# First matrix of the last MLP as seven products of 256 columns, with its weight sums made during the second mixer

## The chip, the cores and the metric

The kernel runs on one core of a Trainium2 chip. The metric is the device time of one execution in microseconds (us). Lines such as L231 are lines of the kernel before, unless a sentence says otherwise; in the changed kernel the same code stands one line lower at L232, and further down by more.

The engines are named as the profile names them: PE multiplies matrices, DVE is the vector engine, ACT the scalar engine, POOL is hardly used here, and SP issues the DMAs. Each engine works through its own instructions in the order of the program, and an instruction that waits holds everything behind it on the same engine.

## The reference

A trunk of two layers works on 1024 tokens of width 1024 in fp32. Layer 0 mixes with a matrix memory (mLSTM), layer 1 with latent attention over shared keys and values; each is followed by an MLP of width 4096. Cut to what the change touches:

```python
h = modulate(rmsnorm(x, norm_g[l, 2]), sh2, sc2)      # h * (1 + scale) + shift
y = sqrelu_mlp(h, mlp_w1[l], mlp_w2[l])               # jnp.square(jax.nn.relu(h @ w1)) @ w2
x = x + g2[:, None, :] * rmsnorm(y, norm_g[l, 3])
```

`w1` is 1024 x 4096 and `w2` is 4096 x 1024.

## The kernel before

**Tiles and products.** The tokens go through in two halves of 512, `hfs[0]` and `hfs[1]`. Activations lie with the features on the 128 partitions, so a half is eight blocks `k` of 128 features by 512 tokens. Each fp32 operand is split into a rounded part and a remainder (type fp32r), and one product is three matmuls, low by high, high by low, high by high: `mm3`, L230 to L233. A weight tile is loaded by one DMA into `raw` (L211, 512 KB), cast on ACT to `wh` (L189), and its remainder is made by a subtraction on DVE, `wl` (L190). There are four `raw` buffers, and four pairs of `wh` and `wl`.

**The MLP.** `mlp` (from L967, before the change) makes a list of steps. A step `hidden(f)` makes 128 of the 4096 hidden features: eight `mm3`, that is 24 matmuls of 128 x 512, into one `ps` accumulator, then relu (L962) and square (L963) on ACT, and the split into `hd` (L471 on ACT, L472 on DVE). A step `up` multiplies hidden features by the second matrix: 24 matmuls of 512 columns into a `pm` accumulator, which DVE adds to the output (L198). The last MLP works in groups of four hidden features' blocks; the `up` steps of the group before alternate with the `hidden` steps of the next. Weights are asked for two steps ahead.

**What runs beside what.** The streams are laid out like this: the last layer's MLP on the first half, `mlp(1, hfs[0], ...)`, runs together with the second mixer, `mixer1(hfs[1], ...)`, which is latent, attention, output projection, residual and norm of the second half. Behind that the last MLP, `mlp(1, hfs[1], ...)`, runs alone but for a filler that writes the results out (`all_out`: `x_to_rows`, with transposes at L1577 and copies at L1578, and `rows_out`). `two_streams` interleaves the two generators; a scheduler then orders the instructions of each engine by a model of their times, with those under `high_priority` pulled ahead.

**Attention.** For each pair of heads and queries, PE makes scores into `pm` (L1330 to L1336), DVE takes the maximum (L1340, L1341), ACT the exponential (L1342), DVE the reciprocal and the scaling (L1343, L1344), PE turns the result (L1450) and multiplies by the values. Finished blocks go to DRAM as `oT` (L1471). Keys, queries and values come from DRAM into `k` tiles (L1427 to L1435), issued on SP among the weight loads.

**The end of the mixer.** `post` adds the residual, takes the norm, and `normed` writes the modulated half as eight pairs of high and low tiles (`Split`), one ACT and two DVE instructions for each feature block; the last MLP's products read them.

**Small buffers.** `tma` is a scratch tile of 2 KB for each partition with one buffer, `Cst` a constant tile that the second mixer doesn't read any more once its latent part is done, and `v8` a tile of layer 0 that lies idle in layer 1.

Of the kernel before, what the change touches and what calls it, by code (L numbers as in the profile page):

```python
# [9 lines left out]
F32 = mybir.dt.float32  # L10
# [7 lines left out]
P = 128  # L18
# [64 lines left out]
def kernel(  # L83
# [39 lines left out]
    def k4v(dt=F32, b=512):  # L123
        return k4(dt)[:, :1024].rearrange("p (a b) -> p a b", b=b)
# [104 lines left out]

    def mm3(o, lh, ll, rh, rl, start, stop):  # L230
        nc.tensor.matmul(o, ll, rh, start=start, stop=False)  # L231
        nc.tensor.matmul(o, lh, rl, start=False, stop=False)  # L232
        pe_last[0] = nc.tensor.matmul(o, lh, rh, start=False, stop=stop)  # L233

# [242 lines left out]
    def normed(h, xs_, rstd, A, sh):  # L477

        for k in range(KD):
# [5 lines left out]
            if k % 4 == 3:  # L485
                yield 1

    def along_tokens(dst, y):
# [143 lines left out]
    def qk_in(hf):  # L632
        hf.q = [k4v(), k4v()]
        hf.k = [k4v(), k4v()]
        for p_ in range(4):
# [3 lines left out]
            yield  # L639

    def v_in(hf):
        h = hf.h
        hf.v = []
        last = sb.tile([P, 4, VE], F32, tag="v8", bufs=1, name=f"v8_{next(uid)}")
        nc.gpsimd.memset(last[:, :, 128:VE], 1.0)
        for t in range(4):
# [298 lines left out]

    def mlp(l, hf, y, sizes, rows=False):


        w1, w2, h = mlp_w1[l], mlp_w2[l], hf.h2
        hids = {}  # L950

        def hidden(f):
# [645 lines left out]
    def rows_out(hf, y, B):  # L1598

        xt = []  # L1600
        for t in range(4):
            a = k4v()
            r0 = hf.i * H + t * P
            nc.sync.dma_start(a, xr[r0 : r0 + P, :].rearrange("p (a b) -> p a b", b=512))
            xt.append(a)
        yield
        for t in range(4):
            yt, st = y.t[t], small(4)
            for g in range(2):
                junk = ps()  # L1610
                nc.scalar.activation(junk, yt[:, g], AF.Square, accum_out=st[:, g : g + 1])
# [8 lines left out]
            for g in range(2):  # L1620
                nc.vector.scalar_tensor_tensor(ys[g], ys[g], r, xt[t][:, g], ALU.mult, ALU.add)
                r0 = hf.i * H + t * P
                nc.sync.dma_start(out[0, r0 : r0 + P, ts(g, 512)], ys[g])
            yield

# [129 lines left out]

    def post(hf, y, B, src, A, sh):
# [5 lines left out]
        yield 0  # L1762
        hf.h2 = Split()
        yield from normed(hf.h2, y, rstd, A, sh)
# [128 lines left out]


    z1 = FH(claim=True)
    ya = [None, None]

    def mixer1(hf, z, attention):
# [5 lines left out]
        yield "fill"  # L1904
        yield from lat
        yield next(att)
        yield from att
# [5 lines left out]
        yield 1  # L1913
        yield from post(hf, y, B2, x_cols, A3, adac(1, SH2))
# [6 lines left out]
    u1 = FH(claim=True)  # L1921

# [10 lines left out]
    v = None  # L1933
    dense = mlp(1, hfs[1], u1, [4] * 8, True)
    while (d := go(dense)) is not end:
# [32 lines left out]
```

## Time and profile before

| | |
|---|---|
| median of three runs | 2376.94 us (2375.88 to 2378.69) |
| the profiled execution | 2377.5 us, of which the span is 2375.5 us |
| granted TensorE clock, mean | 0.997 |
| PE busy | 2343.4 us in 11621 matmuls |
| DVE busy | 1549.6 us |
| ACT busy | 1055.6 us |
| last MLP (second half) | about 2000 us to the last matmul at 2366.6 us |

The span is what the profiler saw of the execution, from the first instruction to the last; 2.0 us of the execution's time lie outside it. A matmul's duration in the trace overlaps with the next one's, so the rate of a stream of matmuls is read from the starts, not from the durations. "A <- B" in a view of waits says that engine and line A waited until B was done.

### The profile page before, as it was taken

To read this page: it belongs to the slowest core of one execution; us is meant where nothing else is said; L and a number is where in the kernel's file an instruction comes from. 1 tells how busy PE (TensorE), PEld (TensorE's weight loads), DVE (VectorE), ACT (ScalarE), POOL (GpSimd) and SP (SyncE) were. 2 spreads that over 40 slices of the span, in tenths; PEclk is the share of its full clock that TensorE was granted. 3 is DMA by queue.
4 is the path that set the end of the run, shared out by engine and by line. 5 is a ranking of instruction groups with operands and counts; after the bars stand their busy time and mean duration, and the time that the engine had idled before them with its cause. 6 is when DMAs were issued, how large, how long until landed. Compare 5 with 4: busy or idle time off the path is not lost.

```text
span 2375.5 us, 30534 instructions
## 1 busy us (share of the span) xinstructions
PE 2343.4 (99%) x11621; PEld 1946.7 (82%) x11621; DVE 1549.6 (65%) x2435; ACT 1055.6 (44%) x1716; POOL 18.2 (1%) x93
## 2 busy tenths in 40 slices
PE   7999999999999999999999999999999999999998
PEld 5888888788888888888888888888888888888887
DVE  6667866868666667877764967765666486353345
ACT  4355334655333454434443554444444453444333
POOL 1000000000000000000000000000000000000000
PEclk9999999999999999999999999999999999999999
DMA  9452664544664745555543454874434354364431
GB/s 313 149 142 85 186 181 139 168 133 144 186 181 143 250 135 187 160 161 183 182 133 113 147 166 163 249 248 136 148 98 143 114 169 129 102 191 140 144 102 62
DMA packets 377106, 374.48 MB, mean 158 GB/s; under 512 B 24355, under 2 KB 282464, under 8 KB 376960
## 3 DMA queue, kind: packets, MB, share of 16 engines
q1 hardware_dynamic: 376672, 372.44, 50.3%
q8 instruction: 91, 1.49, 0.3%
q14 instruction: 55, 0.45, 0.1%
q0 software_dynamic: 288, 0.10, 0.0%
HBM read 313.24 MB, written 59.24 MB: 157 GB/s over the span
## 4 chain that ended last, share of the span: by engine, by line
PE 89%; DVE 4%; DMA 4%; ACT 1%; issue 1%; SPq 0%; DVEq 0%; ACTq 0%
PE ps L231 16%; PE ps L233 16%; PE ps L232 16%; PE pm L231 9%; PE pm L232 9%; PE pm L233 9%; PE pc L1450 1%; DMA raw<-in_a_w_in_dram 1%; DMA raw<-in_mlp_w_dram 1%; PE pc L231 1%; PE pc L233 1%; PE pc L232 1%; PE pm L1336 1%; DVE wl L190 1%; PE pm L820 1%
## 5 line engine op out<-in xcount | busy, mean ns | idle before, releaser
L190 DVE TENSOR_TENSOR wl<-raw,wh 128x1024 fp32r<-128x1024 f32 (+2 forms) x366 | 438.9, 1202 | 442.7 <-ACT wh L189 435.7
L189 ACT CAST wh<-raw 128x1024 fp32r<-128x1024 f32 (+2 forms) x366 | 377.6, 1035 | 704.3 <-PE ps L231 381.7
L231 PE MATMUL ps<-k,wl 128*128 128x512 f32 x1528 | 605.2, 396 | 2.5 <-ACT k L679 1.4
L233 PE MATMUL ps<-k,wh 128*128 128x512 f32 x1528 | 596.1, 390 | 0.0
L232 PE MATMUL ps<-k,wh 128*128 128x512 f32 x1528 | 595.6, 390 | 0.0
L231 PEld LDWEIGHTS ps<-k,wl 128*128 128x128 f32 x1528 | 287.0, 188 | 65.1 <-issue 2.9
L233 PEld LDWEIGHTS ps<-k,wh 128*128 128x128 f32 x1528 | 286.8, 188 | 61.7 <-issue 0.5
L232 PEld LDWEIGHTS ps<-k,wh 128*128 128x128 f32 x1528 | 287.2, 188 | 58.8 <-issue 1.7
L198 DVE TENSOR_TENSOR k<-k,pm 128x512 f32<-128x512 f32 (+1 forms) x254 | 211.0, 860 | 104.1 <-PE pm L233 103.6
L231 PE MATMUL pm<-hd,wl 128*128 128x512 f32 x512 | 200.9, 392 | 0.5 <-ACT hd L471 0.5
L232 PE MATMUL pm<-hd,wh 128*128 128x512 f32 x512 | 199.3, 390 | 0.2 <-DVE hd L472 0.2
L233 PE MATMUL pm<-hd,wh 128*128 128x512 f32 x512 | 199.2, 389 | 0.0
L231 PE MATMUL pm<-wh,hd 128*128 128x512 f32 x488 | 192.2, 394 | 1.6 <-ACT raw L1342 1.3
L232 PE MATMUL pm<-wl,hd 128*128 128x512 f32 x488 | 190.9, 391 | 0.0
L233 PE MATMUL pm<-wh,hd 128*128 128x512 f32 x488 | 190.2, 390 | 0.0
L359 DVE SCALAR_TENSOR_TENSOR tma<-raw,cond,tma 128x512 f32<-128x512 f32 x168 | 125.6, 748 | 20.4 <-DMA raw<-in_kv_ada_w_dram 14.4
L472 DVE TENSOR_TENSOR hd<-tmp,hd 128x512 fp32r<-128x512 f32 x128 | 88.3, 690 | 54.7 <-ACT hd L471 54.4
L1342 ACT ACTIVATE raw<-pm,sm 128x128 f32<-128x128 f32 (+3 forms) x64 | 47.5, 742 | 150.1 <-DVE sm L1341 121.8
L231 PEld LDWEIGHTS pm<-hd,wl 128*128 128x128 f32 x512 | 96.2, 188 | 20.8 <-ACT hd L471 0.9
L232 PEld LDWEIGHTS pm<-hd,wh 128*128 128x128 f32 x512 | 96.1, 188 | 20.5 <-DVE hd L472 0.5
L233 PEld LDWEIGHTS pm<-hd,wh 128*128 128x128 f32 x512 | 96.1, 188 | 20.2
L231 PEld LDWEIGHTS pm<-wh,hd 128*128 128x128 f32 x488 | 91.6, 188 | 22.3 <-ACT raw L1342 3.5
(354 smaller groups left out, 3426.2 us busy)
## 6 DMA issues: line engine op xcount, KB each, us to landing
raw<-in_mlp_w_dram SPq DMA_DIRECT2D x256, 512.0 KB, 4.2
raw<-in_ada_w_dram SPq DMA_DIRECT2D x80, 512.0 KB, 4.2
raw<-in_a_w_in_dram SPq DMA_DIRECT2D x48, 512.0 KB, 4.8
xs<-k SPq DMA_DIRECT2D x40, 256.0 KB, 4.8
raw<-in_kv_ada_w_dram SPq DMA_DIRECT2D x16, 512.0 KB, 4.0
raw<-in_a_w_out_dram SPq DMA_DIRECT2D x16, 512.0 KB, 4.8
kd<-k SPq DMA_DIRECT2D x32, 256.0 KB, 3.8
vd<-k SPq DMA_DIRECT2D x32, 256.0 KB, 4.5
```

The source lines that it names most:

```text
L189: nc.scalar.copy(hi[:, :n], r[:, :n])
L190: i = nc.vector.tensor_sub(lo[:, :n], r[:, :n], hi[:, :n].bitcast(F32))
L198: return f(*a, **k)
L231: nc.tensor.matmul(o, ll, rh, start=start, stop=False)
L232: nc.tensor.matmul(o, lh, rl, start=False, stop=False)
L233: pe_last[0] = nc.tensor.matmul(o, lh, rh, start=False, stop=stop)
L359: nc.vector.scalar_tensor_tensor(acc, r[:, kk], cond[:, k : k + 1], acc, ALU.mult, ALU.add)
L472: nc.vector.tensor_sub(lo, u, hi.bitcast(F32))
L820: nc.tensor.matmul(nv[:, r, i], hf.PT[p_][:, r, cs], v[2 * p_ + r], start=g == 0, stop=True,)
L1336: nc.tensor.matmul(o[:, :w], qh, kh, start=False, stop=True)
L1342: nc.scalar.activation(pr[:, :n], f, AF.Exp, bias=m, scale=SCALE, accum_out=l)
L1450: nc.tensor.transpose(pt[:, ts(2 * e + i, P)], u.prs[i][:, ts(b + e, P)], ident)
```

## The change

The first matrix of the last MLP isn't multiplied block by block any more. Its input is cut in two by feature (1024 = 2 x 512) and in two by token (512 = 2 x 256), a pair of hidden blocks gives two times two blocks of weights, and Strassen's scheme in Winograd's form gets the four result blocks from seven block products in place of eight. A block product is four `mm3`, that is twelve matmuls of 128 x 256. So a pair of hidden blocks takes 7 x 12 = 84 matmuls of 256 columns, where two `hidden` steps took 48 matmuls of 512 columns. All 16 pairs together: 768 matmuls of 512 columns go, 1344 of 256 come.

**Accumulators.** One `ps` accumulator per pair, `u.b`, is used again and again: product 1 goes in, ACT copies it out, product 6 is added on top, ACT copies that out, product 5 is added, DVE reads it, product 3 is added, and ACT takes the relu. Products 2, 7 and 4 use `pc`. `second` writes 6 before 7; the scheduler swaps them at some pairs of the first groups.

**Operand sums.** The scheme needs four sums of weight blocks for each pair. `weight_sums` makes them beside the second mixer: for each of 16 pairs it loads four blocks of 256 KB, makes four additions or subtractions of 128 x 512 on DVE, and stores four sums of 256 KB to a DRAM scratch `sums`. It uses `tma` for the first and the last of the four, so that the second load into it follows the first store from it, and the next pair's first load follows the last store. `with_sums` lets it go on by one part at each step of `mlp(1, hfs[0])`. For the second half `normed_kept` and `quarters` stand in the place of `normed`: the 8 remainders on DVE go, and 14 casts of 128 x 512 on ACT and 22 subtractions on DVE come, for the seven operands of the activations. Three of the seven operands (`rest`) are made at step 61 of `mlp(1, hfs[0])`, when `h2` of the first half sets its buffers free.

**Weights of the last MLP.** A pair loads 512 KB of `mlp_w1`, two times 512 KB of `sums` and 256 KB of `mlp_w1`: 3.5 tiles to cast and to split where two `hidden` steps had 2.

**Order of steps.** The group's four `up` steps go to: behind `first`, `second` and `fourth` of its first pair, and behind `first` of its second pair. The first group has none, having no group before it.

**Output rows.** `rows_out` reads its rows one by one instead of four at once; its scratch for squares is a `tmc` in place of a `ps`.

```diff
+            for p_ in range(NF // 2):            # weight_sums(w), cut
+            get(a11, 0, 0)
+            get(a21, 1, 0)
+            get(a22, 1, 1)
+            yield
+            nc.vector.tensor_sub(a11, a11, a21)
+            nc.vector.tensor_add(a21, a21, a22)
+            put(1, a11)
+            put(2, a21)
+            yield
+            nc.vector.tensor_sub(a22, a22, a11)
+            put(0, a22)
+            a12 = tma()
+            get(a12, 0, 1)
+            yield
+            nc.vector.tensor_sub(a12, a12, a22)
+            put(3, a12)
...
+            def product(i, o, w, start=False):
+                (wh, wl), (bh, bl) = w, B[i]
+                for k in range(4):
+                    mm3(o, wh[:, k], wl[:, k], bh[k], bl[k], start and k == 0, k == 3, more=not start)
...
+            def first(w):
+                u.b, u.x, u.s, u.r = cut(ps()), cut(pc()), tmp(), tmp()
+                product(1, u.b, w[0], True)
+                    nc.scalar.copy(u.s1, u.b)
+                product(2, u.x, w[1], True)
+                    nc.vector.tensor_add(c, u.s1, u.x)
+                    nc.scalar.activation(c, c, AF.Relu)
+            def second(w):
+                product(6, u.b, w[0])
+                    nc.scalar.copy(u.s16, u.b)
+                product(7, u.z, w[1], True)
+                    nc.scalar.copy(u.s7, u.z)
+            def third(w):
+                product(5, u.b, w[0])
+                    nc.vector.tensor_add(u.r[:, N:], u.s7, u.b)
+            def fourth(w):
+                product(4, u.z, w)
+                    nc.vector.tensor_add(cut(u.r), u.s16, u.z)
+                    nc.scalar.activation(u.r, u.r, AF.Relu)
+                    finish(2 * p_ + 1, u.r)
+                product(3, u.b, u.w3)
+                    nc.scalar.activation(u.s[:, N:], u.b, AF.Relu)
+                    finish(2 * p_, u.s)
...
-            for i in range(G):
+            for i in range(0, G if B else 0, 2):
+                four = pair(fs[i] // 2)
+                for part in (four[:1], four[1:2], four[2:]):
+                    steps += part
+                    if part is not four[2:] and done < len(prev):
+                        steps.append(up(prev, done, False))
+                        done += 1
+            for i in range(0 if B else G):
                 steps.append(hidden(fs[i]))
...
-    two_streams(mlp(1, hfs[0], u0, [2] * 16, True), mixer1(hfs[1], z1, attention_second))
+    two_streams(
+        with_sums(mlp(1, hfs[0], u0, [2] * 16, True)), mixer1(hfs[1], z1, attention_second)
+    )
...
-    dense = mlp(1, hfs[1], u1, [4] * 8, True)
+    dense = mlp(1, hfs[1], u1, [4] * 8, True, B)
```

`part is not four[2:]` is always true, since a new slice is another object; so an `up` step may follow behind each of the three parts as long as the group before has one left.

**SP in the second mixer.** One store of `oT` to the next, near the end of attention. Before:

```order
L1471 DMA oT<-tmp_15013 128x256
L211 DMA raw_15148<-in_mlp_w_dram 128x8x128
L1435 DMA k_2719_15397<-vd 128x1024
L1435 DMA k_2720_15398<-vd 128x1024
L1471 DMA oT<-tmp_15180 128x256
```

The same place in the changed kernel, up to the second of these stores:

```order
L978 DMA sums<-tma_17123 128x512
L975 DMA v_451_2640<-in_mlp_w_dram 128x4x128
L975 DMA tma_17176<-in_mlp_w_dram 128x4x128
L978 DMA sums<-tma_17176 128x512
L978 DMA sums<-Cst 128x512
L978 DMA sums<-v_451_2640 128x512
L975 DMA tma_17279<-in_mlp_w_dram 128x4x128
L211 DMA raw_15255<-in_mlp_w_dram 128x8x128
L978 DMA sums<-tma_17279 128x512
L1574 DMA k_2736_15514<-vd 128x1024
L1574 DMA k_2737_15515<-vd 128x1024
L1610 DMA oT<-tmp_15287 128x256
```

Among the weight load and the two loads of values stand eight DMAs of one pair's sums; each store waits for a subtraction on DVE, and everything behind it on SP waits with it.

**DVE at the same place.** Two softmaxes (L1340 to L1344) between weight remainders (L190). Before:

```order
L198 TENSOR_TENSOR k_2072_11984<-k_2072_11984,pm_15053 128x512
L472 TENSOR_TENSOR hd_15082<-pc_15083,hd_15081 128x512
L472 TENSOR_TENSOR hd_15082<-pc_15090,hd_15081 128x512
L1340 TENSOR_REDUCE sm_15120<-pm_15107 128x1
L1341 TENSOR_SCALAR sm_15120<-sm_15120 128x1
L1340 TENSOR_REDUCE sm_15141<-pm_15128 128x1
L1343 RECIPROCAL sm_15121<-sm_15121 128x1
L1341 TENSOR_SCALAR sm_15141<-sm_15141 128x1
L1344 TENSOR_SCALAR raw_15119<-raw_15119,sm_15121 128x640
L1343 RECIPROCAL sm_15142<-sm_15142 128x1
```

In the changed kernel, from the first subtraction of a pair's sums (L983) to the last one (L993):

```order
L983 TENSOR_TENSOR tma_17176<-tma_17176,Cst 128x512
L984 TENSOR_TENSOR Cst<-Cst,v_451_2640 128x512
L473 TENSOR_TENSOR hd_15189<-pc_15190,hd_15188 128x512
L473 TENSOR_TENSOR hd_15189<-pc_15197,hd_15188 128x512
L988 TENSOR_TENSOR v_451_2640<-v_451_2640,tma_17176 128x512
L1479 TENSOR_REDUCE sm_15227<-pm_15214 128x1
L1480 TENSOR_SCALAR sm_15227<-sm_15227 128x1
L1479 TENSOR_REDUCE sm_15248<-pm_15235 128x1
L1482 RECIPROCAL sm_15228<-sm_15228 128x1
L1480 TENSOR_SCALAR sm_15248<-sm_15248 128x1
L1483 TENSOR_SCALAR raw_15226<-raw_15226,sm_15228 128x640
L993 TENSOR_TENSOR tma_17279<-tma_17279,v_451_2640 128x512
```

The four operations of a pair's sums stand between the softmax operations; the last one, which waits for a store of `tma` and the load behind it, stands ahead of the second softmax's reciprocal.

**ACT in the last MLP.** Two `hidden` steps with an `up` between, before:

```order
L189 CAST wh_17914<-raw_17912 128x1024
L962 ACTIVATE tmp_17904<-ps_17879 128x512
L963 ACTIVATE tmp_17904<-tmp_17904 128x512
L471 CAST hd_17878<-tmp_17904 128x512
L189 CAST wh_17920<-raw_17918 128x1024
L189 CAST wh_17960<-raw_17958 128x1024
```

In the changed kernel, the second pair of a group, from the copy of product 1 (L1028) to the relu at L1068 behind product 4:

```order
L1028 COPY tmc_19324<-ps_19308 128x256
L472 CAST hd_19281<-tmp_19139 128x512
L472 CAST hd_19298<-tmp_19138 128x512
L189 CAST wh_19369<-raw_19367 128x1024
L1033 ACTIVATE tmp_19310<-tmp_19310 128x256
L1042 COPY tmc_19386<-ps_19308 128x256
L189 CAST wh_19404<-raw_19402 128x512
L1046 COPY tmc_19400<-pc_19373 128x256
L189 CAST wh_19437<-raw_19435 128x1024
L189 CAST wh_19443<-raw_19441 128x1024
L189 CAST wh_19462<-raw_19460 128x1024
L1068 ACTIVATE tmp_19311<-tmp_19311 128x512
```

Copies of the accumulator (L1028, L1042) are now in one queue with weight casts, and product 6 and product 5 go into the accumulator only behind these copies.

More of the change, by code (lines that the diff above doesn't have):

```diff
@@ L228, with mm3 @@
     pe_last = [None]
[L230 to L233, printed above, removed]
+    def mm3(o, lh, ll, rh, rl, start, stop, more=False):
+        m = dict(skip_group_check=True) if more else {}
+        nc.tensor.matmul(o, ll, rh, start=start, stop=False, **m)
+        nc.tensor.matmul(o, lh, rl, start=False, stop=False, **m)
+        pe_last[0] = nc.tensor.matmul(o, lh, rh, start=False, stop=stop, **m)
     nc.scalar.preload_act_table_set("natural_log_exp_and_others")
@@ L486, in normed, with split_wide, normed_kept @@
                 yield 1
+    def split_wide(hi, lo, u):
+        nc.scalar.copy(hi, u)
+        nc.vector.tensor_sub(lo, u, hi.bitcast(F32))
+    def normed_kept(y, rstd, A, sh):
+        for k in range(KD):
+            with paced():
+                nc.vector.scalar_tensor_tensor(
+                    y[k], y[k], A[:, k : k + 1], rstd, ALU.mult, ALU.mult
+                )
+                nc.scalar.activation(y[k], y[k], AF.Identity, bias=sh[:, k : k + 1])
+            if k % 4 == 3:
+                yield 1
     def along_tokens(dst, y):
@@ L639, in qk_in @@
             yield
+    v8_of = []
     def v_in(hf):
@@ L1609, in rows_out @@
             for g in range(2):
-                junk = ps()
+                junk = tmc()
                 nc.scalar.activation(junk, yt[:, g], AF.Square, accum_out=st[:, g : g + 1])
@@ L1762, in post @@
         yield 0
+        if kept:
+            yield from kept(y, rstd)
+            return
         hf.h2 = Split()
@@ L1892, with quarters, part, rest @@
     rope_perm()
+    B = {}
+    later, sums_on = [None], [False]
+    def quarters(y, rstd):
+        q = lambda kh, th, j: y.t[2 * kh + j][:, :, ts(th, 256)]
+        sub = nc.vector.tensor_sub
+        def part(i, kh, th):
+            t = [k4v(F32R, 256), k4v(F32R, 256)]
+            for j in range(2):
+                s = ts(j, 2)
+                split_wide(t[0][:, s], t[1][:, s], q(kh, th, j))
+            B[i] = [[a[:, k] for k in range(4)] for a in t]
+        yield from normed_kept(y, rstd, A3, adac(1, SH2))
+        part(1, 0, 0)
+        part(2, 1, 0)
+        yield 1
+        for j in range(2):
+            sub(q(0, 0, j), q(0, 1, j), q(0, 0, j))
+        part(3, 1, 1)
+        for j in range(2):
+            sub(q(0, 1, j), q(1, 1, j), q(0, 1, j))
+            sub(q(1, 1, j), q(1, 1, j), q(0, 0, j))
+        part(6, 1, 1)
+        for j in range(2):
+            sub(q(1, 0, j), q(1, 0, j), q(1, 1, j))
+        def rest():
+            part(7, 0, 1)
+            part(5, 0, 0)
+            part(4, 1, 0)
+        later[0] = rest
+        yield 1
     z1 = FH(claim=True)
@@ L1913, in mixer1, with with_sums @@
         yield 1
-        yield from post(hf, y, B2, x_cols, A3, adac(1, SH2))
+        yield from post(hf, y, B2, x_cols, A3, adac(1, SH2), quarters if hf.i else None)
     two_streams(mlp(0, hfs[1], z1, [2] * 14 + [4]), mixer1(hfs[0], z0, attention_first), bg_rest())
     u0 = FH(claim=True)
-    two_streams(mlp(1, hfs[0], u0, [2] * 16, True), mixer1(hfs[1], z1, attention_second))
-    u1 = FH(claim=True)
+    def with_sums(g):
+        bg = weight_sums(mlp_w1[1])
+        n = 0
+        for v in g:
+            if v != "within":
+                n += 1
+                if sums_on[0]:
+                    next(bg, None)
+                if n == 61:
+                    drain(bg)
+                    later[0]()
+            yield v
+    two_streams(
+        with_sums(mlp(1, hfs[0], u0, [2] * 16, True)), mixer1(hfs[1], z1, attention_second)
+    )
+    u1 = FH()
     def all_out():
```

67 lines of the change are left out of this document (61 added, 6 removed).

## The prediction

> **What bounds the kernel.** The page comes first: span, busy times, and the chain that ended last.
>
> ```profile
> span 2375.5 us, 30534 instructions
> PE 2343.4 (99%) x11621; PEld 1946.7 (82%) x11621; DVE 1549.6 (65%) x2435; ACT 1055.6 (44%) x1716; POOL 18.2 (1%) x93
> PE 89%; DVE 4%; DMA 4%; ACT 1%; issue 1%; SPq 0%; DVEq 0%; ACTq 0%
> ```
>
> PE is busy for 99% of the span and makes 89% of the chain, so only fewer or shorter matmuls can shorten the time much, and any new wait of PE is paid in full. The change has two places: the second mixer, where the weight sums are made (they stand in the order beside rows that the trace has between about 1461 and 1744 us), and the last MLP (2000 us to the end). The view of windows gives both; its columns are the stretch, its length, each engine's busy time, the granted clock, the DMA share and GB/s.
>
> ```profile
> 1480.00:1600.00 120.00, 119.51 (x587) 100.24 (x586) 82.79 (x126) 50.32 (x79) 0.62 (x3) 1.00 0.76 251
> 1600.00:1740.00 140.00, 138.12 (x788) 118.29 (x787) 85.39 (x142) 59.77 (x106) 1.85 (x9) 1.00 0.45 147
> 1900.00:2000.00 100.00, 100.00 (x445) 81.99 (x444) 78.45 (x110) 47.46 (x68) 0.39 (x4) 1.00 0.50 153
> 2000.00:2100.00 100.00, 100.00 (x452) 82.48 (x451) 35.19 (x39) 42.52 (x62) 0.00 (x0) 1.00 0.38 114
> 2100.00:2200.00 100.00, 100.00 (x449) 82.03 (x448) 53.54 (x90) 44.47 (x77) 0.00 (x0) 1.00 0.55 169
> ```
>
> PE is full in all of them, at full clock. In the last MLP DVE and ACT are at about half, so each has room on average. The view of PE's waits from 1500 to 2010 us has three rows and from 2000 us on none:
>
> ```profile
> PE pm L231 <- ACT raw L1342: 1.3, 2, 1.1
> PE pm L1332 <- DMA k<-td: 0.5, 1, 0.5
> PE pc L1450 <- DVE raw L1344: 0.4, 2, 0.2
> ```
>
> Nothing can be won back from waits here: what the change gains must come from the stream of matmuls, and each wait that it makes is a loss.
>
> **Term 1, the stream.** How fast matmuls follow each other is read from the timeline, by starts. The first two rows bound 53 steps of 512 columns in the last MLP, the next two 38 steps of 256 columns in an early projection, all of them with a weight load for each matmul.
>
> ```profile
> 2249.83 0.39 PE L231 MATMUL ps<-k,wl 128*128 128x512 f32 x1
> 2261.85 0.39 PE L233 MATMUL ps<-k,wh 128*128 128x512 f32 x1
> ...
> 311.00 0.28 PE L233 MATMUL ps<-wh,k 128*128 128x256 f32 x1
> 315.56 0.28 PE L232 MATMUL ps<-wl,k 128*128 128x256 f32 x1
> ```
>
> 12.02 / 53 = 0.2268 us and 4.56 / 38 = 0.1200 us. A 256 costs 0.529 of a 512, not half, so seven eighths of the work cost 84 x 0.1200 = 10.08 us where 48 x 0.2268 = 10.89 us went: 0.81 us for each pair, and for all 768 x 0.2268 - 1344 x 0.1200 = 174.2 - 161.3 = **-12.9 us**. An ideal eighth would be 21.8 us; the fixed part of a short matmul eats 8.9 of it.
>
> The Trainium skill, page "TensorE: Matmul & The Clock Gate", section "Back-to-back issue gap", gives a warm spacing of N / 2.4 + 2.5 ns, so 215.8 and 109.2 ns. By that the term would be 165.7 - 146.7 = 19.0 us; the trace shows 226.8 and 120.0 ns, so it doesn't agree and the sum goes by the trace.
>
> **Term 2, waits in the last MLP.** The groups by line and form give the prices (busy, then mean ns of one, then idle time before):
>
> ```profile
> L189 ACT CAST wh<-raw 128x1024 fp32r<-128x1024 f32 x350 | 366.9, 1052 | 694.5 <-PE ps L231 381.3 <-DMA raw<-in_mlp_w_dram 103.6 <-PE pm L231 73.7
> L190 DVE TENSOR_TENSOR wl<-raw,wh 128x1024 fp32r<-128x1024 f32 x350 | 426.9, 1222 | 438.1 <-ACT wh L189 433.5 <-PE ps L233 2.7 <-DMA lw<-wl 1.0
> L471 ACT CAST hd<-tmp 128x512 fp32r<-128x512 f32 x128 | 79.5, 621 | 3.4
> L472 DVE TENSOR_TENSOR hd<-tmp,hd 128x512 fp32r<-128x512 f32 x128 | 88.3, 690 | 54.7 <-ACT hd L471 54.4
> L881 ACT COPY hd<-pc 128x256 f32<-128x256 f32 x32 | 9.6, 387 | 0.1
> ```
>
> A pair's own work on ACT is three casts of 1024 and one of 512 (3.8 us), three copies and two relus of 256 (1.9), a relu, two squares and two casts of 512 (some 3.1): about 8.8 us; on DVE three remainders and a half (4.3), two of 512 (1.4) and three additions of 256 (an estimate of 0.4 each from the copy's 0.39): about 6.9. An `up` adds 1.05 to ACT and 1.22 + 1.3 to DVE. With its ups a group (41.9 us of PE) asks 21.8 us of ACT and 23.9 of DVE, so the average is covered. Locally it isn't: the second pair of a group runs 6, 7, 5, 4, 3 and the next pair's 1 and 2 with no `up` between, 10.1 us in which ACT has about 8.8 of its own, and the first group, which has no ups, is 20.2 us with 17.6 us of ACT beside the leftovers of the handover. Product 5 may start only when ACT has copied the accumulator behind product 6, and product 3 only behind DVE's addition; one other product of twelve matmuls, 1.44 us, lies between. The copy takes 0.39; if a weight cast of 1.05 has just begun ahead of it, 1.05 + 0.39 is all of that 1.44, and the passage of the signal is paid: in the last matmul's rows, next, the reader starts 0.42 us after the matmul's start, 0.19 beyond its 0.23 of streaming.
>
> ```profile
> 2366.57 0.39 PE L233 MATMUL pc<-wh,hd 128*128 128x512 f32 x1
> 2366.99 0.69 DVE L198 TENSOR_TENSOR k<-k,pc 128x512 f32<-128x512 f32 x1 [0.30 <-PE pc L233]
> ```
>
>  Bounds: nothing, if the scheduler's order suits; and one such miss of 1.05 at both places for all 16 pairs, 34 us, if it never does. I take 0.3 us a pair, nearer to nothing since a cast can stand ahead of the copy only part of the time: **+4.5 us**, with 3 to 11 as the likely part of the bounds.
>
> **Term 3, the second mixer.** The queue's row and four kinds of transfers (KB, then median us from issue to landing):
>
> ```profile
> q1 hardware_dynamic: 376672, 372.44, 50.3%
> raw<-in_mlp_w_dram SPq DMA_DIRECT2D x256, 512.0 KB, 4.2
> tmc<-xs SPq DMA_DIRECT2D x32, 256.0 KB, 4.0
> xr<-tmc SPq DMA_DIRECT2D x16, 256.0 KB, 2.4
> out_dram<-tmc SPq DMA_DIRECT2D x16, 256.0 KB, 2.1
> L1471 SPq DMA_DIRECT2D oT<-tmp x12: 319/339/1548, 1601.6 to 1775.9; - x12
> ```
>
> The sums add 64 loads and 64 stores of 256 KB, 33.5 MB. At q1's rate (50.3% of 2375.5 us for 372.44 MB, 3.2 us of all engines for each MB) that is about 108 us, in a stretch of 283 us whose share was (120 x 0.76 + 140 x 0.45) / 260 = 0.59: it goes to 0.97. DVE gets 64 x 0.69 = 44 us more in that stretch, where it was 61 to 69% busy, so 77 to 85%. SP gets 128 issues of about 0.34 us.
>
> The chain of a pair of sums is serial, since `tma` is one buffer: subtraction 0.69, store 2.1 to 2.4, load up to 4.0, two issues of 0.34; 6.0 to 7.8 us for one hop (an estimate from these rows; the low end takes 2.5 for a load, since it is half of the 512 KB that take 4.2), and two hops a pair. In the attention part one pair stands from one `oT` store to the next, (1775.9 - 1601.6) / 11 = 15.8 us by before, so the chain of 12.0 to 15.6 us just fits. But the places of the two waits aren't even. These rows of DVE and PE show one of them:
>
> ```profile
> 1735.35 1.28 DVE L198 TENSOR_TENSOR k<-k,pm 128x512 f32<-128x512 f32 x2
> ...
> 1741.67 0.55 DVE L1344 TENSOR_SCALAR raw<-raw,sm 128x640 f32<-128x640 f32 x1
> 1742.89 0.16 DVE L1343 RECIPROCAL sm<-sm 128x1 f32<-128x1 f32 x1 [0.67 <-ACT raw L1342]
> 1743.16 0.62 DVE L1344 TENSOR_SCALAR raw<-raw,sm 128x768 f32<-128x768 f32 x1
> ...
> 1744.59 0.60 PE L1450 MATMUL pc<-ident,raw 128*128 128x128 f32 x4
> ```
>
> The pair's first subtraction now stands behind the row at 1735.35 (done 1736.6), its last one behind the row at 1741.67 (done 1742.2) and ahead of the reciprocal at 1742.89. That leaves 5.6 us for a hop of 6.0 to 7.8; what is over holds the reciprocal and the scaling up, and PE's transposes at 1744.59, which had 0.8 us left after 1743.78. So a hop at its slow end costs PE about 1.4 us here, one at its quick end nothing. DVE's weight remainders queue there too, but SP's loads run up to four tiles ahead. Bounds: nothing, and 16 pairs times 1.4 to 2 us, 22 to 32 us. I take **+3 us**, two or three misses, near the quick end, because PE waited only 2.2 us in this whole stretch before and the scheduler spread the sums over 16 places.
>
> The Trainium skill, page "DMA: Bandwidth & Descriptors", section "Anatomy of one DMA — SWDGE (gpsimd) path", fits 2.0 us + bytes / 436e3 to a DMA, for the software path: 2.6 us for 256 KB, so a hop of about 6.6 us by it, inside the bounds. The trace's stores at 2.1 to 2.4 agree roughly, its loads of 4.0 don't.
>
> **The rest at nothing.** `quarters` adds 14 casts (8.7 us of ACT) and 14 operations of DVE (9.7 us) near 1900 to 2000 us; DVE has 21.5 us free in that window, ACT 52, and PE has `up` steps of the first half ahead. If the handover isn't covered, the part after the norm is seen, up to 3 us. The last MLP's 1.5 tiles more for a pair add 12.6 MB in 365 us at a share of 0.38 to 0.55: about 40 us, hidden. The output path behind the last matmul stays as it is.
>
> **The sum.** -12.9 + 4.5 + 3 = -5.4 us. The profiled execution took 2377.5 us (2375.5 of span and 2.0 outside it), 0.6 above the median of the runs, so the forecast is 2376.9 - 5.4 = **2371.5 us**. A change of 0.2%, 4.75 us, is about what a measurement of this kernel can tell from no change.
>
> **Rivals.**
> - *Gain given back in the last MLP.* Waits of 0.5 to 0.8 us a pair (8 to 13 us) leave a result within 0.2%: about 2375. For it: three more casts and copies in ACT's queue for each pair, and the rows of waits (ACT's casts waited 103.6 us on late loads in the kernel before, as the group of L189 shows). Against it: ACT is at half on average.
> - *Slower: the sums' chain paces the second mixer.* In DVE's and SP's order a late load holds up softmaxes, remainders and weight loads. It takes the 8.4 us that the other terms leave when all 16 pairs lose 0.5, at a hop of 5.6 + 0.8 + 0.5 = 6.9 us. With loads of 256 KB at 4.0 us, at a DMA share near 1.0, the hop is 7.8: 16 times 1.4 us = 22 us, less 8.4, +14 us: 2391. For it: 0.97 of DMA share, and loads at 4.0 us under only 0.5. Against it: the chain fits on average, and 6 of the 16 pairs stand before 1600 us at wide distances.
> - *No waits at all.* -12.9 us gives 2364.
> - *The stream gains nothing* (accumulating onto a `ps` that was read makes each block restart): every block product would pay some 0.1 us, 112 x 0.1 = 11 us; 2375 to 2380. No row speaks for it.
>
> **Chances.** Forecast, with part of the waits (2364 to 2372): 0.40. Within 0.2%: 0.25, the first rival and mild cases of the second. Slower: 0.35, nearly all of it the chain of sums. Range 2363 to 2391, the likeliest case's own 2364 to 2373.
>
> **What would show it.** Right: in the last MLP blocks of 256 start every 0.120 us, the last MLP is some 8 us shorter, and PE's waits there name copies of `ps` and additions on DVE by 3 to 11 us in all. The mixer shows PE's waits on DVE's softmax scaling or on ACT's exponential by a few us between 1461 and 1744 us. Wrong: the stretch of the mixer grows by over 10 us with DVE waiting for loads of `tma`; or products start later than 0.120 us apart without a wait.

## The result and the profile after

The changed kernel takes 2439.19 us (median of four runs, 2438.32 to 2441.07) against 2377.72 us: a ratio of 1.0261, interval 1.0243 to 1.0278. It is slower by 61 us, where the forecast was 5 us faster. The profiled span grows from 2375.5 to 2436.5 us, by 61.0 us too. One execution of `sums_only`, a kernel of the experiments, took 9680.71 us in place of some 2427 and is left out of its time.

The page of the changed kernel, in the parts shown of the kernel before:

```profile
span 2436.5 us, 32383 instructions
PE 2351.7 (97%) x12197; PEld 1974.3 (81%) x12197; DVE 1640.4 (67%) x2593; ACT 1098.7 (45%) x1826; POOL 17.9 (1%) x89
```

PE has 576 matmuls more and 8 us more of busy time, but its share fell from 99% to 97%: most of the 61 us is PE doing nothing. The windows say where first; these two are stretches of the second mixer.

```profile
1480.00:1600.00 120.00, 106.09 (x493) 87.81 (x494) 87.09 (x135) 44.11 (x70) 0.21 (x1) 0.96 0.93 302
1600.00:1740.00 140.00, 120.46 (x645) 101.03 (x644) 87.13 (x146) 49.55 (x86) 1.64 (x8) 0.96 0.72 230
```

In the mixer PE was busy for 119.5 of 120 and 138.1 of 140 us before; now for 106.1 and 120.5, and the granted clock is 0.96 there. Rows of PE's timelines split the loss. Before, the last `up` step of the first half (`pm`) ends and the first `hidden` step of the last MLP (`ps`) begins here:

```profile
2010.65 0.39 PE L233 MATMUL pm<-wh,hd 128*128 128x512 f32 x1
2010.87 0.39 PE L231 MATMUL ps<-k,wl 128*128 128x512 f32 x1
```

In the changed kernel these are the first and the last matmul of the last MLP:

```profile
2060.39 0.28 PE L232 MATMUL ps<-k,wl 128*128 128x256 f32 x1
...
2426.95 0.39 PE L234 MATMUL pc<-wh,hd 128*128 128x512 f32 x1
```

Before, the last matmul started at 2366.57. So **+49.5 us** came ahead of the last MLP, **+10.9 us** in it (366.6 us in place of 355.7), and 0.6 us behind it. The last MLP, which was to be some 8 us shorter, is 10.9 us longer.

**The second mixer.** PE's waits between 1460 and 1800 us, and then DVE's and SP's there (waiter, released by: us, times, longest):

```profile
PE pc L1589 <- DVE raw L1483: 14.3, 8, 3.9
PE pm L232 <- ACT raw L1481: 8.4, 4, 3.8
```

```profile
DVE tma L983 <- DMA tma<-in_mlp_w_dram: 22.9, 11, 4.5
DVE tma L993 <- DMA tma<-in_mlp_w_dram: 19.6, 12, 3.8
```

```profile
SPq L978 <- DMA tma<-in_mlp_w_dram: 57.6, 25, 4.9
SPq L975 <- DMA sums<-tma: 38.2, 16, 5.1
```

These two rows are 22.7 of some 40 us that PE waits there. PE waits for the softmax (L1483 is the scaling, L1481 the exponential), DVE waits for the loads of the sums, and SP waits for loads and stores of the sums for some 96 us. One such wait on DVE's timeline, from a maximum of a softmax to its reciprocal and beyond:

```profile
1708.64 0.82 DVE L1479 TENSOR_REDUCE sm<-pm 128x1 f32<-128x640 f32 x1
...
1712.17 0.69 DVE L983 TENSOR_TENSOR tma<-tma,Cst 128x512 f32<-128x512 f32 x1 [2.53 <-DMA tma<-in_mlp_w_dram]
1712.78 0.15 DVE L1482 RECIPROCAL sm<-sm 128x1 f32<-128x1 f32 x1
...
1719.25 0.69 DVE L993 TENSOR_TENSOR tma<-tma,v 128x512 f32<-128x512 f32 x1 [2.35 <-DMA tma<-in_mlp_w_dram]
1719.86 0.15 DVE L1482 RECIPROCAL sm<-sm 128x1 f32<-128x1 f32 x1
```

The subtraction of the sums (L983) stands ahead of the reciprocal (L1482) and waits 2.53 us for its load; so does L993 for the second softmax. PE's row for the transposes behind it:

```profile
1720.73 1.54 PE L1589 MATMUL pc<-ident,raw 128*128 128x128 f32 x6 [3.86 <-DVE raw L1483]
```

How long the chain through `tma` is shows in its first and last operation:

```profile
1466.15 0.69 DVE L983 TENSOR_TENSOR tma<-tma,Cst 128x512 f32<-128x512 f32 x1 [2.94 <-DMA Cst<-in_mlp_w_dram]
...
1521.17 0.69 DVE L983 TENSOR_TENSOR tma<-tma,Cst 128x512 f32<-128x512 f32 x1 [4.45 <-DMA tma<-in_mlp_w_dram]
1536.59 0.69 DVE L993 TENSOR_TENSOR tma<-tma,v 128x512 f32<-128x512 f32 x1 [2.98 <-DMA tma<-in_mlp_w_dram]
...
1793.11 0.69 DVE L993 TENSOR_TENSOR tma<-tma,v 128x512 f32<-128x512 f32 x1 [1.75 <-DMA tma<-in_mlp_w_dram]
```

A hop is the way from one of these operations to the next through `tma`: subtraction, store, load. 31 hops take 1793.11 - 1466.15 = 327 us, 10.5 us each; a single one took 15.4 us (1521.17 to 1536.59), and the longest 30.3 us (1585.85 to 1616.11). At 23 of the 31 DVE stood and waited for the load into `tma`. The rows beside which they stand took 283 us in the kernel before (1461 to 1744 us, as in the prediction): 44 us less, nearly the loss of this stretch.

**The last MLP.** Its products run as fast as forecast; the first and the last row below stand 23 starts apart, (2246.73 - 2243.97) / 23 = 0.120 us. Then comes a wait, here product 3 behind DVE's addition (L1054), which stands behind a weight remainder:

```profile
2243.97 0.28 PE L232 MATMUL ps<-k,wl 128*128 128x256 f32 x1
...
2246.73 0.28 PE L234 MATMUL pc<-k,wh 128*128 128x256 f32 x1
2247.61 0.38 PE L232 MATMUL ps<-k,wl 128*128 128x256 f32 x1 [0.61 <-DVE tmp L1054]
```

```profile
2246.01 1.22 DVE L190 TENSOR_TENSOR wl<-raw,wh 128x1024 fp32r<-128x1024 f32 x1
2247.15 0.41 DVE L1054 TENSOR_TENSOR tmp<-tmc,ps 128x256 f32<-128x256 f32 x1
```

PE's waits there in all:

```profile
PE pm L232 <- DVE hd L473: 9.4, 7, 4.9
PE ps L232 <- DVE tmp L1054: 2.4, 4, 0.6
...
PE ps L232 <- ACT tmc L1042: 1.5, 2, 0.7
```

The greatest item, 9.4 us, is at steps of the second matrix that wait for hidden features (`hd`). The view counts less than is lost, since a stalled PE starts again slowly, as the last section shows: summed over starts, what lies beyond 0.227 and 0.120 us for each matmul is 22.2 us in this MLP, and 2.7 us in that of the kernel before. The filler's transposes, of which 16 more fall into this MLP, take 8.2 us by starts in place of 4.0. With the 12.9 us that the shorter stream saves this gives the difference: 19.5 + 4.2 - 12.9 = 10.8 us.

### The profile page after: what moved, and what is told of

It is laid out like the page before. It is cut to its first block, busy times and chain, and to the rows that moved or that the text cites. A ratio compares the mean times of both kernels' runs of the same rounds, so it can differ in the third digit from the quotient of the medians.

```text
span 2436.5 us, 32383 instructions
## 1 busy us (share of the span) xinstructions
PE 2351.7 (97%) x12197; PEld 1974.3 (81%) x12197; DVE 1640.4 (67%) x2593; ACT 1098.7 (45%) x1826; POOL 17.9 (1%) x89
## 5 line engine op out<-in xcount | busy, mean ns | idle before, releaser
L190 DVE TENSOR_TENSOR wl<-raw,wh 128x1024 fp32r<-128x1024 f32 (+3 forms) x398 | 469.0, 1181 | 359.2 <-ACT wh L189 349.1
L189 ACT CAST wh<-raw 128x1024 fp32r<-128x1024 f32 (+3 forms) x398 | 403.9, 1018 | 639.9 <-PE ps L232 230.9
L232 PE MATMUL ps<-k,wl 128*128 128x512 f32 (+1 forms) x1528 | 578.7, 379 | 8.5 <-DVE tmp L1054 2.4
L233 PE MATMUL ps<-k,wh 128*128 128x512 f32 (+1 forms) x1528 | 569.8, 373 | 0.0
L234 PE MATMUL ps<-k,wh 128*128 128x512 f32 (+1 forms) x1528 | 569.2, 372 | 0.0
L198 DVE TENSOR_TENSOR k<-k,pm 128x512 f32<-128x512 f32 (+1 forms) x254 | 210.7, 858 | 109.7 <-PE pm L234 109.4
L232 PE MATMUL pm<-wh,hd 128*128 128x512 f32 x488 | 196.7, 403 | 20.2 <-DVE hd L473 9.4
L234 PE MATMUL pm<-wh,hd 128*128 128x512 f32 x488 | 193.0, 396 | 0.0
L1481 ACT ACTIVATE raw<-pm,sm 128x128 f32<-128x128 f32 (+3 forms) x64 | 47.5, 742 | 167.1 <-DVE sm L1480 144.9
```

What stands on the lines that cost most here:

```text
L189: nc.scalar.copy(hi[:, :n], r[:, :n])
L190: i = nc.vector.tensor_sub(lo[:, :n], r[:, :n], hi[:, :n].bitcast(F32))
L198: return f(*a, **k)
L232: nc.tensor.matmul(o, ll, rh, start=start, stop=False, **m)
L233: nc.tensor.matmul(o, lh, rl, start=False, stop=False, **m)
L1481: nc.scalar.activation(pr[:, :n], f, AF.Exp, bias=m, scale=SCALE, accum_out=l)
```

## The experiments

Times are medians beside runs of the kernel before on the same chip, with the ratio's interval where there were several runs. The kernel before had medians of 2377.7 to 2380.1 us in these batches, so a difference of 2 or 3 us between kernels of different batches says little. "The change" is the changed kernel.

**The two parts by themselves.** `no_sums` leaves out the making of the weight sums; its last MLP loads as many bytes of `mlp_w1` in the places of the sums, so its products are of other operands:

```diff
-                return lambda: pieces(
-                    wload([(0, 0, by_k(sums[p_][:, 2 * i * H : 2 * (i + 1) * H]))], P)
-                )
+                return lambda: pieces(wload([(0, 0, wcols(w1, (2 * p_ + i) * P))], P))
...
-                if sums_on[0]:
-                    next(bg, None)
...
-                    drain(bg)
```

> The changed kernel without the making of the weight sums: nothing is added to the second mixer, and the last MLP loads blocks of mlp_w1 in the places of the sums (as many bytes), so its products are of other operands. Theory: the loss has two separate parts, about +47 us up to the first product of the last MLP and +13.6 us in the last MLP; then this takes 2439 - 47 = about 2392 us, and the last MLP starts within 3 us of where it starts before. Rival: the last MLP is slow because the mixer leaves it late weights, or the mixer slow because of the other changes (operand sums of the activations); then it takes under 2382 us in the first case, over 2410 in the second.

2389.37 us, ratio 1.0052 (1.0035 to 1.0069). Its last MLP starts at 2008.7 us, 2.2 us earlier than before, and takes 365.6 us. `sums_only` is the kernel before with `weight_sums` and `with_sums` as in the change, and nothing that uses them.

> The kernel before with the weight sums made beside the second mixer as in the change, and not used; the last MLP as before. Theory: the sums alone cost the mixer its +47 us, so about 2425 us. Rival: they cost only together with the new operand sums and the new weight order; then under 2405 us.

2426.93 us, ratio 1.0207 (1.0186 to 1.0227), from three runs. Its last MLP, which is that of the kernel before, starts 49.5 us later and takes the same 355.7 us:

```profile
2060.35 0.39 PE L231 MATMUL ps<-k,wl 128*128 128x512 f32 x1
```

Both forecasts held: the sums cost some 50 us in the kernel before as in the changed one, the new products 12 us, and the two add. The operand sums of the activations cost nothing. (The +47 and +13.6 us that these two expectations name take the 13th matmul of the last MLP before for its first, at 2013.59 us; the split is 49.5 and 10.9 us, as above.)

**Traffic or arithmetic.** `dma_only` takes the change's four operations of DVE out, and `dve_only` is `no_sums` with only these operations, on tiles that no DMA touches:

```diff
-            nc.vector.tensor_sub(a11, a11, a21)
-            nc.vector.tensor_add(a21, a21, a22)
...
-            nc.vector.tensor_sub(a22, a22, a11)
...
-            nc.vector.tensor_sub(a12, a12, a22)
```

> The changed kernel with all loads and stores of the sums on the same buffers, and without the four operations of DVE for each pair; the stored blocks are those loaded. Theory (DVE stands and waits for loads of sums, and the softmax behind it waits with it): with nothing on DVE to wait, most of the 47 us go, 2395 to 2410 us, and PE's waits on the softmax's scaling nearly vanish. Rival (DMA traffic and SP, which waits in its order for each store and load, delay the weights and the keys): still 2425 us or more.

> The kernel no_sums with the 64 operations of 128 x 512 on DVE at the same places of the program, on tiles that no DMA touches. Theory: DVE's added work alone has room, at most 5 us over no_sums. Rival: DVE's load is what holds the softmax up; 20 us or more over no_sums.

`dve_only` took 2389.32 us, nothing over `no_sums`, though the scheduler had put most of its operations ahead of 1600 us, so it shows only that DVE's work has room there. `dma_only` took 2443.89 us in one run: as slow as the change, against my theory. But it wasn't the same experiment any more. With nothing on DVE to pace them, 48 of the 64 stores moved to before 1411 us, and PE's waits are in other places:

```profile
PE pm L232 <- DVE k L198: 21.4, 3, 18.3
PE pm L1465 <- DMA k<-qd: 12.6, 1, 12.6
```

So the chain costs without DVE standing in it too, when it stands in SP's order.

**Places further apart.** `pipelined` gives the fourth block a tile of its own, puts loads, a pause, then operations and stores on three steps of the MLP, and queues them behind what the step has already put on DVE and SP:

```diff
+            a12 = sb.tile([P, H], F32, tag="RM", bufs=1, name=f"a12_{next(uid)}")
...
             get(a22, 1, 1)
+            get(a12, 0, 1)
+            yield
             yield
...
-                    next(bg, None)
...
+                    with tc.issue_after(of(dve)), tc.issue_after(of(sp)):
+                        next(bg, None)
```

> The changed kernel with the weight sums in three parts per pair, one part per step of the MLP: four loads, then a step of nothing, then the four operations of DVE and the four stores; the fourth block has a tile of its own (the idle RM) instead of sharing tma, and the parts are queued on DVE and SP no earlier than the step they belong to. So each load has two steps to land before DVE asks for it. The bytes, the number of DMAs and DVE's work stay. Theory (DVE, in order, stands waiting for loads of sums and the softmax behind it is late): most of the 47 us go, 2395 to 2405 us, DVE's waits on the sums' loads fall from 50 us to under 10. Rival (the traffic itself, a DMA share of 0.9, delays everything): 2425 us or more, with waits on loads of weights, keys and values in place of those on sums.

2415.54 us, ratio 1.0148 (1.0131 to 1.0165): 24 us less than the change, where 34 to 44 were expected. DVE's waits on the sums' loads are gone, all but one of 2.6 us. But three steps a pair reach to 2012 us, into the norm behind the mixer, where DVE's work is the path itself:

```profile
1961.00 1.30 DVE L198 TENSOR_TENSOR k<-k,pm 128x512 f32<-128x512 f32 x2
1964.91 0.69 DVE L986 TENSOR_TENSOR tma<-tma,Cst 128x512 f32<-128x512 f32 x1 [2.61 <-DMA tma<-in_mlp_w_dram]
...
1966.66 0.69 DVE L459 TENSOR_TENSOR tmc<-tmc,tmc 128x512 f32<-128x512 f32 x1
```

PE waits 10.2 us there for that norm's sum (L459):

```profile
PE pc L463 <- DVE tmc L459: 10.2, 1, 10.2
```

`dma_pinned` is `pipelined` without the four operations.

> The kernel pipelined without the four operations of DVE for each pair: loads and stores at the same places, stores of the blocks as they were loaded. In dma_only the stores and loads had moved to 1200 to 1410 us, far ahead of the second mixer's attention, so it didn't test this place; here they are queued behind the step's own loads. Theory: no more than 5 us from pipelined. Rival: if traffic and SP's order cost, as much as pipelined whatever that takes, and over 2415 us.

2387.64 us in one run, as `no_sums`. All the traffic is there, at the same steps of the program, for nothing; a DMA share of 0.86 between 1460 and 1600 us doesn't hurt. It is spread wider than in the change, though: its stores go out between 1491 and 1943 us, those of the change between 1467 and 1794. My forecast was within 5 us of `pipelined`, and it is 28 less: DVE's operations, waiting or in a bad place, and the stores that wait for them on SP, are what still cost in `pipelined`.

**A shorter chain.** `two_tiles` has only the tile of its own and the fourth load beside the other three, no pause and no pinning.

> The changed kernel with a tile of its own (the idle RM) for the fourth block, loaded with the other three: one store and load a pair less in the chain, subtractions still on DVE where the scheduler puts them. Theory: DVE's wait at the last of the four operations (19.6 us in twelve waits) goes, the one at the first (22.9 us and more) stays: 2410 to 2425 us. Rival (what counts is not the chain's length): no less than 2433 us.

2422.86 us in one run, within the forecast: with one hop a pair fewer the last MLP starts 34.5 us later than before in place of 49.5. `pipelined` has this tile too, so of its 24 us about 7 are left for the pause and the pinned places.

**The operations on POOL.** `on_pool` has `nc.gpsimd` in the place of `nc.vector` for the four operations, and nothing else.

> The changed kernel with the 64 subtractions and additions of the weight sums on POOL instead of DVE, and nothing else: the same loads and stores in the same chain on the same buffers, at nearly the same places of SP's order. dve_only showed that DVE's work costs nothing and dma_pinned that the traffic costs nothing; what is left is that DVE, in order, stands waiting for the loads. Theory: on POOL nobody but some clearing of softmax tiles queues behind the wait, so most of the 48 us in the second mixer go: 2390 to 2400 us, PE's waits on the softmax's scaling under 5 us. Rival (the serial chain delays SP, and so keys and weights): 2425 us or more.

2431.44 us, ratio 1.022 (1.0205 to 1.0235). The theory as I had put it fell: DVE is free of the wait, and only 8 us are won. PE waits elsewhere now, and SP's timeline shows why:

```profile
1591.65 0.77 PE L1469 MATMUL pm<-k,k 128*128 128x512 f32 x1 [13.97 <-DMA k<-qd]
```

```profile
1560.67 1.41 SPq L1531 DMA_DIRECT2D kd<-k  x3
1566.94 0.32 SPq L978 DMA_DIRECT2D sums<-tma  x1
1567.35 0.38 SPq L1531 DMA_DIRECT2D kd<-k  x1
1568.31 0.32 SPq L978 DMA_DIRECT2D sums<-Cst  x1
...
1581.88 2.81 SPq L1566 DMA_DIRECT2D k<-kd  x2
1584.78 0.43 SPq L1568 DMA_DIRECT2D k<-qd  x1
```

The store of the keys at 1567.35 stood behind a store of a sum that SP was waiting to issue; the loads of keys and queries follow late. With the wait off DVE, SP holds the mixer up.

**Off both queues.** Two ways: `all_on_pool` is `on_pool` with the sums' loads and stores issued by POOL as well (`nc.gpsimd.dma_start`), with the same chain and no pinned places; `pool_pinned` is `pipelined` with the operations on POOL.

> The kernel on_pool with the sums' loads and stores issued by POOL too, not by SP: the whole serial chain with its hops stands in POOL's order, on the same buffers, at no pinned places. Theory (the chain holds up what is queued with it on SP and DVE): the other queues are free of it, 2386 to 2400 us. Rival (the chain's transfers collide with the weights' and keys' on the DMA engines): 2410 us or more, with waits on weights and queries at unchanged places of SP.

> The kernel pipelined (loads, a step of nothing, then operations and stores; queued no earlier than their step) with the four operations on POOL instead of DVE. on_pool showed that taking the wait off DVE alone moves it: PE then waited 14 us for a load of queries that stood behind the chain on SP. Theory: the loss needs an in-order queue that stands waiting in the chain, first DVE's, then SP's; with the places far enough apart for SP and the operations off DVE neither stands long: 2386 to 2394 us, as dma_pinned. Rival (traffic and POOL's operations cost by themselves): 2410 us or more.

2400.40 us, ratio 1.0084 (1.0068 to 1.0101), and 2396.08 us, ratio 1.0067 (1.0053 to 1.008): 39 and 43 us less than the change, 11 and 7 above `no_sums`; both a little above what was expected. How far above is known only roughly: the ratios say 8 and 4 us, with intervals that just overlap that of `no_sums`, the starts of the last MLP in the traces 17 and 10. In `all_on_pool` the chain waits as before, but on POOL (first column the waiter):

```profile
POOL tma L975 <- DMA sums<-tma: 66.9, 22, 5.2
POOL tma L983 <- DMA tma<-in_mlp_w_dram: 53.8, 14, 6.2
POOL tma L993 <- DMA tma<-in_mlp_w_dram: 47.9, 16, 5.3
```

169 us of waiting there hold back almost nothing else. The chain is even slower here, 369 us for 31 hops (1466.4 to 1835.5), with the same bytes, order and buffers: what costs is mainly which instructions stand behind it. One thing more differs from the change: the page of `all_on_pool` has the sums' 33.7 MB in another DMA queue (`q0 software_dynamic`) than the weights (`q1`), so what the shared queue adds wasn't tried by itself. `dma_pinned` and `pool_pinned` have all of it in `q1`, spread wider.

**The last MLP's order.** `ups_even` is `no_sums` with another order of steps, and product 7 ahead of 6:

```diff
-                for part in (four[:1], four[1:2], four[2:]):
-                    steps += part
-                    if part is not four[2:] and done < len(prev):
+                final = f0 == NF and i == G - 2
+                for j, part in enumerate(four):
+                    steps.append(part)
+                    if j in ((1, 3) if final else (1, 2)) and done < len(prev):
```

> The kernel no_sums (nothing made beside the mixer, products of other operands) with the last MLP's steps in another order: product 7 before 6, one step of the second matrix behind products 7 and 6 and one behind product 5 of each pair, so that each copy of the accumulator has 2.9 us or a whole step of the second matrix before PE needs it; in the last pair one stands behind product 3. Theory (PE waits on the copies and additions between products, 0.6 to 0.8 us at two places of a group, and on the first and last group's hidden features, 5.0 and 2.9 us, which also lowers the clock): of the 23 us of excess in the last MLP 10 to 15 go, 2375 to 2380 us. Rival (the waits come from ACT's and DVE's load in the groups, so they only move): within 4 us of no_sums, 2389.

2380.21 us, ratio 1.0002 (0.9992 to 1.0011): 9 us less than `no_sums`, and 12 by the ratios. The last MLP takes 354.4 us instead of 365.6, and 355.7 in the kernel before. Its waits:

```profile
PE pm L232 <- DVE hd L473: 5.8, 1, 5.8
PE ps L232 <- ACT tmc L1044: 1.5, 2, 0.7
```

The recurring waits of each group and the one at the end are gone; what is left is one stall where the first step of the second matrix waits for the first group's hidden features. `fill_slow` lets the filler on at every second step only.

```diff
         if v != "last" and d != "within":
-            v = next(fill)
+            n += 1
+            if n % 2 == 0:
+                v = next(fill)
```

> The kernel ups_even with the filler that writes the first half's rows out let on at every second step of the last MLP only, instead of every step: its work on ACT and DVE is the same, but thinner in the first two groups. ups_even has one stall left in the last MLP, at the first step of the second matrix, 5.9 us and 1.4 us of lower clock behind it. Theory (the filler's squares and products stand in ACT's and DVE's order between the first hidden features): 4 to 8 us less than ups_even, 2372 to 2376 us. Rival (casts of 3.5 weight tiles a pair fill ACT by themselves): within 2 us of ups_even.

2375.29 us, ratio 0.9982 (0.9973 to 0.9992), and the stall is gone. With weight sums for nothing, the new products gain 0.2%.

**All together.** Three complete kernels: `both` (sums as in `pipelined`, steps as in `ups_even`), `pool_all` (sums as in `on_pool`, steps and filler as in `fill_slow`), and `best` (sums as in `pool_pinned`, steps and filler as in `fill_slow`).

> The change complete, with the sums as in pipelined and the last MLP's steps as in ups_even; it computes what the change computes. Theory: pipelined and ups_even add, so pipelined less 10 to 15 us: 2380 to 2395 us. Rival: under 2377 us would mean that the sums cost nothing once DVE doesn't wait.

> The change complete, with the sums on POOL as in on_pool, the steps as in ups_even and the filler as in fill_slow; it computes what the change computes. Theory: the gains add, on_pool less 9 to 18 us, 2375 to 2385 us; if the sums on POOL cost nothing at all, 2372 to 2376 us, under the 2379 us of the kernel before. Rival: over 2390 us.

> The change complete, with the sums as in pool_pinned, the steps of the last MLP as in ups_even and the filler as in fill_slow. Theory: as fill_slow with free sums, 2373 to 2379 us, at or just under the kernel before. Rival: over 2385 us.

`both`: 2401.86 us, ratio 1.0096 (1.0081 to 1.0111); it missed its range, which counted on a faster `pipelined`, while the gain over `pipelined`, 14 us, is as expected. `pool_all`: 2417.95 us, ratio 1.0165 (1.015 to 1.018); my forecast for it rested on a cheap `on_pool` and fell with that. `best`: 2382.39 us, ratio 1.0007 (0.9998 to 1.0016), 57 us less than the change and level with the kernel before, 3 us above its forecast. The parts add, but no complete version here beats the kernel before: the 6 us that the sums still cost (1.0007 against 0.9982) are more than the 4 that `fill_slow` gains.

## Why the prediction was wrong

**Term 1, the stream, was right.** 256 columns start every 0.120 us in the changed kernel too.

**Term 3 is the step that failed.** It said +3 us, with 22 to 32 as the upper bound; the runs show 49 to 50 us (`sums_only`, and the 49.5 us of the changed kernel's trace). The mechanism was the one of the second rival, "the sums' chain paces the second mixer", which had 0.35; its price was too low by more than half, for two reasons. First, the hop: I added transfers and issues as rows of quieter stretches have them, 6.0 to 7.8 us. The hops took 10.5 us on average. For 26 of them the trace has both landings, and there 8.8 of 10.6 us are the work itself, the subtraction with its 0.7 us, the store and the load, and 1.8 us are waits in order, on SP ahead of the store and the load and on DVE ahead of the subtraction. The store into `sums` took 3.8 us on average from issue to landing, where I had 2.1 to 2.4, the load into `tma` 4.4, where I had 2.5 to 4.0; the waits in order I had at nothing. The medians seem harmless, but the longest are two and a half to four times as long. All stores of sums (L978), then all loads for them (L975):

```profile
DMA to landing us min/median/max: 2.0/2.7/11.0
```

```profile
DMA to landing us min/median/max: 2.7/4.2/10.6
```

So two hops need 17.6 us without any wait in order, and the 15.8 us from one `oT` store to the next, which I had for them, aren't enough: "the chain just fits" was wrong by itself.

Second, I priced each place by itself, as if what is late at one place were made up before the next. In this chain through one buffer little is made up: at 23 of 31 hops DVE came to the subtraction before its load had landed, and the queues that hold the late hops push back the softmax, the keys and the queries. My reason for the quick end, that PE had waited only 2.2 us in this stretch before, says nothing of a chain that wasn't there.

What the chain does is shown by moving it: one hop a pair fewer, -16 us; with places further apart as well, -24; off DVE alone, -8 with SP in its place; off DVE and SP by issuing from POOL, -39; at pinned places, one hop fewer and off DVE, -43. The transfers alone, spread somewhat wider, cost nothing (`dma_pinned`).

**Term 2 was mis-sized.** It said +4.5 us with 3 to 11 as the likely part; the last MLP has 19.5 us more beyond the pure stream than before and 4.2 us more at the filler's transposes, so it is 10.9 us longer in place of 8 shorter. The place that I named, a copy or addition behind a weight cast or remainder between two products, is there, at 2.4 and 1.5 us. What I left out of the sum were the hidden features at the ends of groups: an `up` stood one product step behind the pair that feeds it, and none of it was priced. That is the 9.4 us on `hd`, with the slow restart behind the two long ones. `ups_even` takes 9 to 12 us away by order alone and `fill_slow` 5 more.

**The rest at nothing held.** In `no_sums` the last MLP starts 2.2 us earlier than before, `quarters` and all, and in the changed kernel's last MLP PE waits for no load of weights.

**Rivals.** That waits in the last MLP give the gain back had its time at 2375; by itself it came out at 2389. The stream that gains nothing is refuted by the 0.120 us, and the case without waits by the 22.2 us. The signs that I named for being wrong, a mixer longer by over 10 us and DVE waiting for loads of `tma`, are what the profile shows.

**What stays open.** What the sums still cost on POOL, some 4 to 17 us by the three ways of reading it, isn't settled. DVE's own operations get longer there, as the next section shows, but whether that is all of it wasn't tried.

## What to carry to other kernels

Work that is hidden in bytes and in busy time can still be a chain: count its hops, give each hop the transfer times under the traffic that it will meet (here 8.2 us where quieter rows had 4.6 to 6.4) and the waits in the in-order queues on its way (here 1.8 us), and compare the sum with the time between the places that the order leaves it. Put such a chain where nobody queues behind it, or far apart enough that each load lands before its reader's turn; taking the wait off one of two queues here only moved it to the other. And when a step is cut into smaller products on one accumulator, the long steps that used to hide the handling between them have to be dealt out again, one for each reuse.

## What was not expected of the hardware

A long wait of PE costs more than itself. After 4.86 us of nothing the first two of PE's matmuls of 512 columns start 0.60 us apart, the next five steps are 0.43 and one is 0.33 before they are back at 0.23, some 1.5 us more than at the full rate; the first and the last of them are in these rows of the changed kernel:

```profile
2140.59 0.80 PE L232 MATMUL pm<-wh,hd 128*128 128x512 f32 x1 [4.86 <-DVE hd L473]
...
2142.47 0.63 PE L233 MATMUL pm<-wl,hd 128*128 128x512 f32 x1
2142.89 0.63 PE L234 MATMUL pm<-wh,hd 128*128 128x512 f32 x1
2143.32 0.49 PE L232 MATMUL pm<-wh,hd 128*128 128x512 f32 x1
```

The Trainium skill, page "TensorE: Matmul & The Clock Gate", section "What's actually happening", has the array at half its clock after an idle window of about 3.4 us; the 0.43 us for 0.23 agree with that.

POOL's operations on two tiles slow down some of DVE's. In `all_on_pool` a weight remainder takes 2.31 us in the place of 1.22 while POOL works on two tiles:

```profile
1627.05 2.31 DVE L190 TENSOR_TENSOR wl<-raw,wh 128x1024 fp32r<-128x1024 f32 x1
```

```profile
1626.79 1.49 POOL L984 TENSOR_TENSOR Cst<-Cst,v 128x512 f32<-128x512 f32 x1
```

Nine remainders that ran beside such an operation for over 40% of their time took 1.82 us on average, 48 that ran beside none 1.22. DVE's additions of an accumulator (L198, `k<-k,pm`) took 0.68 us beside POOL and without. Such an operation of 128x512 takes 1.3 to 1.5 us on POOL here (1.49 in this row) where DVE takes 0.69. The Trainium skill, page "GPSIMD Engine Reference", section "1. Specifications", says that POOL shares its interfaces to SBUF, the memory in which the tiles lie, with DVE, and that DVE's instructions contend for them when they have two inputs in SBUF or run in a mode with two ports. The times of these two agree, since a remainder reads two tiles, and such an addition one tile and an accumulator, which the kernel keeps in PSUM. The softmax's scaling, which reads one tile, gets longer too, 1.76 us in place of 0.62 at 1625.37 us; whether that is the mode with two ports no run here shows.
